# First queries, keys and pooling by 256-column products read by parity, with other places for the pooling weights and a later bias table

## The chip, the cores and the metric

The kernel runs on one core of a Trainium2 chip. The metric is the device time of the program in microseconds. The engines are PE (matrix products, with its own weight loads), ACT, DVE, POOL and SP; SP and POOL also issue transfers (DMA).

## The reference

A bidirectional encoder of two layers over 256 tokens of 1024 channels, in float32. Each layer has two parts:

```python
def _token_mixer(xn, w_in, w_pool, pool_scale, w_a, w_b, w_o, rel_bias):
    u, q, k, v, g_pool, g_attn = jnp.split(xn @ w_in, SPLITS, axis=-1)
    ug = u.reshape(B, S, POOL_GROUPS, POOL_GROUP_DIM)
    pooled = jnp.stack([_centred_mean(ug[:, :, gi], w) for gi, w in enumerate(POOL_WINDOWS)], axis=2) - ug
    pool_out = jnp.einsum('bsgc,gcd->bsgd', pooled, w_pool).reshape(B, S, POOL_WIDTH) * pool_scale
    ...
    for gi, (window, dilation) in enumerate(ATTN_GROUPS):     # (128, 1), (512, 4), (2048, 16), 4 heads each
        ...
        bias = rel_bias[buckets][:, hs].T
        o_g, lse_g = _dilated_group(q[:, :, hs], k[:, :, hs], v[:, :, hs], bias, window, dilation)
    ...
    merged = jax.nn.sigmoid(g_pool) * (pool_out @ w_a) + jax.nn.sigmoid(g_attn) * (attn_out @ w_b)
    return merged @ w_o

def _conv_ffn(xn, w_up, conv_w, conv_b, w_down):
    a, gval = jnp.split(xn @ w_up, 2, axis=-1)
    ...                                                      # depthwise convolution of width 3 on a
    return (jax.nn.gelu(a) * gval) @ w_down
```

Both parts are added to the stream after an RMS norm at their entry, and a last RMS norm ends the program.

## The kernel before

Every float32 operand of a large product is split into a high part, rounded to `fp32r`, and a low part, the rest. A product is then three: high by high, high by low, low by high. The tokens are kept by parity: axis `t` holds even and odd tokens, axis `m` the 128 of each.

The weights are streamed. The class `Weights` holds a list of loads (`add`) and a list of pieces in the order of use (`use`). A load is mostly 1 MB into one of three `raw` buffers, cut into two pieces; a load with a `tag` goes to an idle place named by that tag instead. Opening a piece is a cast on ACT (`wh`, L215) and a subtraction on DVE (`wl`, L216), into one of five pairs of buffers; pieces are opened up to three ahead of the one in use. `load(upto)` issues loads on SP's queue, and `due` says how far ahead that goes.

One layer of the mixer runs as follows. `by_rows` computes 512 columns over four pieces, 48 products of 512 columns, for the pooling branch (`u`), then for two sets of queries and keys (`qk1`, `qk2`): 24 pieces. Its results lie with tokens on the partitions, so they are transposed in blocks on DVE and their blocks exchanged by 16 transfers on POOL's queue (`cross`). After each piece `early` is called; it counts the pieces, moves the exchanges on, and from pieces 15, 17, 19 and 21 on runs the four pooling groups (`pool`: copies of `u` on ACT, running sums on DVE, a split in high and low). Then come eight projections (`proj`, in two pairs of queries and keys for the first head group), and after each of the first four a part of the pooling product (`pool_out`, 12 products). From the seventh on, scores and the rest of the attention are mixed in.

In `proj` the high and low parts of `x` are one operand of 512 columns:

```python
        for k in range(nk):
            nc.tensor.matmul(ps, wh(k), x2[:, k], start=(k == 0), stop=False)
        for k in range(nk):
            nc.tensor.matmul(ps[:, 1], wl(k), x2[:, k, 0], start=False, stop=(k == nk - 1))
```

so two sums come out, and its eviction needs one ACT and two DVE instructions. In other places (`moving`, L90) an operand is read with its two halves in alternation.

In layer 0 only, `load_bias` and `build_bias` make the table `bt` of the attention's position bias: three products from a one-hot matrix (`ohr`, in place `m2`), copies to `fsb`, three transfers to DRAM (`fd`) and five back (`bt`), all on POOL's queue. `build_bias` is a generator that `early` steps, one step for each count above 1: after pieces 2, 3 and 4 a product each, then the transfers. The instruction order on PE, ACT and DVE is that of the source from the end of `u` on; before that, and on POOL and SP throughout, a planner sets it.

Of the kernel before, what the change touches and what calls it, by code (L numbers as in the profile page):

```python
# [10 lines left out]
F32 = mybir.dt.float32  # L11
F32R = mybir.dt.float32r
AF = mybir.ActivationFunctionType
ALU = mybir.AluOpType
AX = mybir.AxisListType

P = 128
D = 1024
S = 256
DEPTH = 2  # L20
KD = D // P
# [12 lines left out]
NT = 5  # L34
# [76 lines left out]
class Weights:  # L111
# [42 lines left out]
    def load_by(self, n):  # L154
# [10 lines left out]
        for c in range(0, shape[0], step):  # L165
            self.nc.sync.dma_start(out=t[:, c : c + step], in_=src[:, c : c + step])
            yield

    def queue_behind(self, insts, n):

        self.behind, self.n_behind = insts, self.n_split + n

    def _split(self, upto):
        nc = self.nc
        self.load(self.due)
        first = self.n_split
        while self.n_split < len(self.pieces):
            i = self.n_split
            n, cut, shape, slot = self.pieces[i]
            if i >= upto and (slot is None or i >= max(upto, first + 2) or i >= upto + 4 or i < 4):  # L180
                break
            if slot is None and len(self.live) == self.BUFS:
                break
            self.load(n + 1)
            with ExitStack() as queued:
                if i < self.n_behind:
                    for inst in self.behind:
                        queued.enter_context(self.tc.issue_after(inst.ins))
                for part in self.open_next():
                    for make in part:  # L190
                        make()
            self.due = n + self.RAW

    def open_next(self):

# [50 lines left out]
def encoder(ctx, tc, x, w_in, w_pool, pool_scale, w_a, w_b, w_o, norm1, norm2, w_up, conv_w,  # L246
# [29 lines left out]
    for l in range(DEPTH):  # L276
        if l == 0:
            slots = (("m2", 0, 2), ("m2", 1, 2), ("ybig",), ("at2",))
            for j in range(2):
                kept = rows(w_in[l], j * 512, 4, C_V, 512)  # L280
                more = rows(w_in[l], j * 512, 4, C_V + 512, 512, "k1" if j else None)
                for n in range(2):
                    W.use(kept[n : n + 1], slots[2 * j + n : 2 * j + n + 1])
                    W.use(more[n : n + 1])
            W.n_scaled = len(W.pieces)
        else:
            W.use(rows(w_in[l], 512, 4, C_V, 512), (("ybig",), ("at2",)))
            for j in range(2):
                W.use(rows(w_in[l], j * 512, 4, C_V + 512, 512))

        def half_of(w, c0, half, n):
            for j in range(n):
                W.use(rows(w, j * 512, 4, c0 + half.start, 512))

        for half in HALVES:
            half_of(w_in[l], 0, half, 2)
        for c0 in (C_Q + 512, C_K + 512, C_Q + 1024, C_K + 1024):
            half_of(w_in[l], c0, HALVES[0], 2)
        for c in PAIRS:
            q = cols(w_in[l], C_Q + c * 256)  # L300
            k = cols(w_in[l], C_K + c * 256)
            if c == 0:
                pool = W.add(
                    w_pool[l].rearrange("g (k p) c -> p (g k) c", p=P), (8, 256),
                    [((lambda t, j=j: t[:, 4 * j : 4 * j + 4, :]), (4, 256)) for j in range(2)],
                )
                q.insert(1, pool[0])
                k.insert(1, pool[1])
            W.use(q + k)
        half_of(w_in[l], C_V + 1024, HALVES[0], 2)  # L310

        for half in HALVES:
            half_of(w_in[l], C_GP, half, 2)
        for half in HALVES:
            half_of(w_a[l], 0, half, 2)
            half_of(w_in[l], C_GA, half, 2)
            half_of(w_b[l], 0, half, 1)
        for c in range(4):
            W.use(rows(w_o[l], c * 256))
        slots = (("v1",), ("ybig",), ("at2",))  # L320
        for kind, n in ORDER.split():
            n = int(n)
            if kind == "v":
                if l + 1 < DEPTH:
                    W.use(rows(w_in[l + 1], 0, 4, C_V, 512), (("m2", 0, 2), ("m2", 1, 2)))
                continue
            for j in range(2):
                if kind == "d":
                    W.use(rows(w_down[l], (4 * n + 2 * j) * P))
                elif kind == "r":  # L330
                    src = w_up[l][j * 512 : (j + 1) * 512].rearrange("(k p) c -> p k c", p=P)
                    c0 = (4 * n * P, 4 * n * P + DFF)
                    W.use(
                        W.add(
                            tuple(src[:, :, c : c + 256] for c in c0), (4, 2, 256),
                            [
                                ((lambda t, j=j: t[:, 2 * j : 2 * j + 2].rearrange("p k h c -> p k (h c)")), (2, 512))
                                for j in (0, 1)
                            ],
                        )  # L340
                    )
                else:
                    p = rows(w_up[l], j * 512, 4, (kind == "g") * DFF + 4 * n * P, 512)
                    W.use(p, slots[2 * j : 2 * j + 2] if (kind, n) == ("a", 0) else ())
        W.use(rows(w_down[l], (NF - 2) * P))
# [76 lines left out]
    def load_bias():  # L422
# [14 lines left out]
        nc.vector.tensor_sub(  # L437
            out=rr[64:96], in0=rb[64:96], in1=rr[64:96].bitcast(F32)
        )
        ohr = big.tile([P, NT * 256], F32R, tag="m2", name="onehot_r")  # L440
        nc.scalar.copy(out=ohr, in_=oh)
        return rr, ohr

    def build_bias(rr, ohr):

        fsb = big.tile([96, NT * 256], F32, tag="q1", name="fsb")
        for c0, groups in ((0, (0, 0)), (512, (0, 1)), (1024, (2,))):
            width = 256 * len(groups)
            ps = acc.tile([P, 512], F32, tag="acc", name="f_ps")
            nc.tensor.matmul(ps[:, :width], rr, ohr[:, c0 : c0 + width], start=True, stop=True)  # L450
            for j, g in enumerate(groups):
                cc = slice(j * 256, (j + 1) * 256)
                rows = slice(32 * g, 32 * g + HPG)
                nc.vector.tensor_copy(fsb[rows, c0 + j * 256 : c0 + (j + 1) * 256], ps[rows, cc])
            yield
# [92 lines left out]

    def chunk_mm(ps, wh, wl, xh, xl, nk):

        for k in range(nk):
            nc.tensor.matmul(ps, wh(k), xh[:, k], start=(k == 0), stop=False)
            nc.tensor.matmul(ps, wh(k), xl[:, k], start=False, stop=False)
            nc.tensor.matmul(ps, wl(k), xh[:, k], start=False, stop=(k == nk - 1))

    def two_sums(ps, wh, wl, x2, nk):


        for k in range(nk):
            nc.tensor.matmul(ps, wh(k), x2[:, k], start=(k == 0), stop=False)  # L560
        for k in range(nk):
            nc.tensor.matmul(ps[:, 1], wl(k), x2[:, k, 0], start=False, stop=(k == nk - 1))

    def proj(x2):

        i, (wh, wl) = W.get()
        flush()
        ps = mmp.tile([P, 2, S], F32, tag="mm", name="proj_ps")
        two_sums(ps, lambda k: wh[:, k, :], lambda k: wl[:, k, :], x2, KD)
        W.free(i)  # L570
        return ps[:, 0], ps[:, 1]

    def halves(a):

        return a.rearrange("p (t m) -> p t m", t=2)

    def in_order(a):

        return a.rearrange("p (m t) -> p t m", t=2)

    def add_up(out, sums):

        nc.scalar.copy(out=out, in_=sums[1])
        nc.vector.tensor_add(out=out, in0=sums[0], in1=out)

    def row_mm(ps, ah, al, wh, wl, first, last):

# [343 lines left out]
    for l in range(DEPTH):  # L931
# [109 lines left out]
        def early():  # L1041
            nonlocal count
            count += 1
            if l == 0 and count > 1:
                next(bias, None)
            if crossing and next(crossing[0], "end") == "end":
                crossing.pop(0)
# [15 lines left out]
        def pool_out(po2):  # L1063
            for j in range(2):
                i, (wh, wl) = W.get()
                for gg in range(2):
                    ph, pl = pooled[2 * j + gg]
                    for oc in range(2):
                        ps = acc.tile([P, 2, P], F32, tag="acc", name="pool_ps")
                        cc = slice(oc * P, (oc + 1) * P)  # L1070
                        chunk_mm(
                            ps, lambda k: wh[:, 2 * gg + k, cc], lambda k: wl[:, 2 * gg + k, cc], ph, pl, 2
                        )
                        c = 4 * j + 2 * gg + oc
# [153 lines left out]
        scaling = scaled_queries()  # L1228
        for c in PAIRS:
            for n in range(4):  # L1230
                src, rest = (halves(a) for a in proj(x2))
                if c == 0:
                    next(pool_parts)
                hd = 2 * c + n % 2
                scale = HD**-0.5 if n < 2 else 1.0
                hi, lo = ((qh, ql) if n < 2 else (kh, kl))

                def evict(hi=hi, lo=lo, hd=hd, scale=scale, src=src, rest=rest):
                    nc.scalar.mul(out=hi[:, hd], in_=src, mul=scale)
                    nc.vector.scalar_tensor_tensor(  # L1240
                        out=lo[:, hd], in0=src, scalar=scale, in1=hi[:, hd].bitcast(F32),
                        op0=ALU.mult, op1=ALU.subtract,
                    )
                    nc.vector.scalar_tensor_tensor(
                        out=lo[:, hd], in0=rest, scalar=scale, in1=lo[:, hd].bitcast(F32),
                        op0=ALU.mult, op1=ALU.add,
                    )

                later.append(evict)
# [305 lines left out]
```

## Time and profile before

| | |
|---|---|
| median of 3 runs | 821.38 us (820.81 to 821.65) |
| the profiled execution | 821.03 us |
| its span, from the first to the last instruction | 819.3 us |
| PE busy | 811.5 us (99%) |
| PE's weight loads busy | 715.0 us (87%) |
| DVE busy | 651.6 us (80%) |
| ACT busy | 481.1 us (59%) |
| POOL busy | 209.5 us (26%) |
| mean granted clock of PE | 0.999 |

A row of a timeline gives the start in us, the time in us, engine, line, operation, output and inputs, shape, how often, and in brackets the idle time before it and what ended that. A row by groups gives line, engine, operation, shapes and count, then busy us in total and mean ns of one. A row of a stretch gives its bounds, its length, and for each engine the busy us with the count of instructions.

### The profile page before, as it was taken

Reading aid. Unit: us, or ns where it says so; the run is one execution under the profiler, and the core shown is the slowest. Engines: PE = TensorE matmul, PEld = TensorE weight load, DVE = VectorE, ACT = ScalarE, POOL = GpSimd, SP = SyncE. Lnnn points to the kernel's source line nnn. Section 1 sums busy time; section 2 is a strip of 40 time slices with the busy share of each in tenths; the row PEclk is TensorE's granted clock in tenths of the full one; section 3 lists DMA queues with packets and bytes.
Section 4 is the critical chain, followed back from the end, with each engine's and each line's share of the span. In section 5 each row is a group of like instructions: output and inputs, shape, how many; then the busy total and the mean of one; then the engine's idle time right before and its main releaser. Section 6 shows DMA issues by size and latency. Waiting matters only on the chain. (4 is left out here: it accounts for less than half of the span.)

```text
span 819.3 us, 11339 instructions
## 1 busy us (share of the span) xinstructions
PE 811.5 (99%) x4030; PEld 715.0 (87%) x4030; DVE 651.6 (80%) x918; ACT 481.1 (59%) x700; POOL 209.5 (26%) x439
## 2 busy tenths in 40 slices
PE   9999999999999999999999999999999999999997
PEld 7888899898888888888888889888888888888886
DVE  6967979667768699989756599796678767999894
ACT  7735475454545577768445456655445447777672
POOL 1153220513012233370000333025030133332501
PEclk9999999999999999999999999999999999999999
DMA  8697585976657888786726776658567487887751
GB/s 316 233 329 227 185 276 169 268 219 220 222 201 237 282 254 256 208 272 211 257 104 212 254 252 201 210 184 258 202 230 258 146 276 237 256 250 236 222 202 52
DMA packets 95164, 186.07 MB, mean 227 GB/s; under 512 B 9774, under 2 KB 26366, under 8 KB 95108
## 3 DMA queue, kind: packets, MB, share of 16 engines
q1 hardware_dynamic: 81956, 160.62, 58.9%
q0 software_dynamic: 12848, 24.43, 10.7%
q8 instruction: 32, 0.52, 0.3%
q10 hardware_dynamic: 304, 0.30, 0.1%
q14 instruction: 24, 0.20, 0.1%
HBM read 160.65 MB, written 1.59 MB: 198 GB/s over the span
## 5 line engine op out<-in xcount | busy, mean ns | idle before, releaser
L216 DVE TENSOR_TENSOR wl<-raw,wh 128x1024 fp32r<-128x1024 f32 x278 | 336.1, 1217 | 112.2 <-ACT wh L215 110.6
L694 PE MATMUL rows_ps<-wh,x 128*128 128x512 f32 x1344 | 405.4, 380 | 0.0
L215 ACT CAST wh<-raw 128x1024 fp32r<-128x1024 f32 x278 | 286.7, 1043 | 141.2 <-PE rows_ps L694 97.0
L694 PEld LDWEIGHTS rows_ps<-wh,x 128*128 128x128 f32 x1344 | 254.1, 189 | 35.6
L694 PE MATMUL rows_ps<-wl,x 128*128 128x512 f32 x672 | 254.7, 379 | 0.0
L694 PEld LDWEIGHTS rows_ps<-wl,x 128*128 128x128 f32 x672 | 127.1, 189 | 17.6
L719 POOL DMA_DIRECT2D up_turned<-up_rows x192 | 94.1, 498 | 164.7 <-DVE up_rows L729 66.0
L588 PE MATMUL res_ps<-wh,actq 128*128 128x512 f32 (+1 forms) x152 | 56.0, 369 | 0.0
L589 PE MATMUL res_ps<-wl,actq 128*128 128x512 f32 (+1 forms) x152 | 55.9, 368 | 0.0
L590 PE MATMUL res_ps<-wh,actk 128*128 128x512 f32 (+1 forms) x152 | 55.9, 368 | 0.0
L719 POOL DMA_DIRECT2D pt<-rows x64 | 31.8, 504 | 80.2 <-ACT wh L215 64.2
L719 POOL DMA_DIRECT2D qk<-qk_rows x64 | 31.3, 497 | 65.6 <-DVE qk_rows L729 30.8
L694 PE MATMUL rows_ps<-wh,po 128*128 128x512 f32 x128 | 39.7, 382 | 0.0
L492 POOL TENSOR_SCALAR ss<-ss 128x1 f32<-128x1 f32 x8 | 1.8, 222 | 133.6 <-ACT junk L488 133.6
L560 PE MATMUL proj_ps<-x,wh 128*128 128x512 f32 x128 | 32.2, 394 | 0.0
L589 PEld LDWEIGHTS res_ps<-wl,actq 128*128 128x128 f32 x152 | 28.8, 189 | 3.7
L588 PEld LDWEIGHTS res_ps<-wh,actq 128*128 128x128 f32 x152 | 28.8, 189 | 3.7
L590 PEld LDWEIGHTS res_ps<-wh,actk 128*128 128x128 f32 x152 | 28.8, 189 | 3.6
L719 POOL DMA_DIRECT2D way<-way x32 | 15.7, 497 | 60.6 <-DVE way L1325 57.9
L719 POOL DMA_DIRECT2D u<-u x32 | 15.8, 502 | 48.4 <-DVE u L729 41.6
L729 DVE STREAM_TRANSPOSE up_rows<-rows_ps 128x512 f32<-128x512 f32 x40 | 26.3, 693 | 2.3 <-PE rows_ps L694 2.3
L1422 ACT ACTIVATE yg<-a,prm 128x256 f32<-128x256 f32 x44 | 26.5, 601 | 1.4
(231 smaller groups left out, 1189.3 us busy)
## 6 DMA issues: line engine op xcount, KB each, us to landing
raw<-in_w_in_dram SPq DMA_DIRECT2D x56, 1024.0 KB, 5.8
raw<-in_w_up_dram SPq DMA_DIRECT2D x40, 1024.0 KB, 5.1
raw<-in_w_down_dram SPq DMA_DIRECT2D x22, 1024.0 KB, 4.8
up_turned<-up_rows POOLq DMA_DIRECT2D x160, 64.0 KB, 5.1
raw<-in_w_a_dram SPq DMA_DIRECT2D x8, 1024.0 KB
raw<-in_w_o_dram SPq DMA_DIRECT2D x8, 1024.0 KB, 4.5
qk<-qk_rows POOLq DMA_DIRECT2D x64, 64.0 KB, 5.0
pt<-rows POOLq DMA_DIRECT2D x64, 64.0 KB, 5.0
```

The source lines that it names most:

```text
L215: lambda: nc.scalar.copy(out=h, in_=src),
L216: lambda: nc.vector.tensor_sub(out=l, in0=src, in1=h.bitcast(F32)),
L492: nc.gpsimd.tensor_scalar_add(ss[:, 3:4], ss[:, 0:1], EPS)
L560: nc.tensor.matmul(ps, wh(k), x2[:, k], start=(k == 0), stop=False)
L588: nc.tensor.matmul(ps, ah, wh, start=first, stop=False)
L589: nc.tensor.matmul(ps, ah, wl, start=False, stop=False)
L590: nc.tensor.matmul(ps, al, wh, start=False, stop=last)
L694: nc.tensor.matmul(ps, x2[:, 2 * n + j, part, t, :], moving(w[:, j], HALVES[0]), start=(n + m == 0), stop=(n == of - 1 and m == 5),)
L719: nc.gpsimd.dma_start(out=out[b, i], in_=in_[a, j])
L729: nc.vector.transpose(out=out[:, :, t].rearrange("p j (a c) r -> p a c j r", a=2), in_=ps[t].rearrange("p (c j r a) -> p a c j r", a=2, c= ...
L1422: nc.scalar.activation(y, aj, AF.Identity, bias=b, scale=w1)
```

## The change

The eight projections and the pooling products use one helper, `chunk_mm`: per 128 channels three products of 256 columns, which read even and odd tokens alternately. One sum comes out, in the order of the tokens, which the eviction reads by parity; its second DVE instruction goes. The pooling weights, one load of 1 MB before, become two of 512 KB, each into an idle place (`q0`, `k0`), and stand in the list of loads ahead of the last two loads of the second key set. `reach` replaces a fixed number of loads ahead: loads to idle places don't count. The one-hot matrix goes to `q0` and `k0` instead of `m2`, in two copies, and the bias steps come for counts above 4 instead of above 1.

```diff
+    def reach(self, n):
+
+        free = self.RAW
+        while n < len(self.loads):
+            free -= self.loads[n][2] is None
+            n += 1
+            if not free:
+                break
+        while n < len(self.loads) and self.loads[n][2] is not None:
+            n += 1
+        return n
...
-            self.due = n + self.RAW
+            self.due = max(self.due, self.reach(n))
...
-        for c0 in (C_Q + 512, C_K + 512, C_Q + 1024, C_K + 1024):
+        for c0 in (C_Q + 512, C_K + 512, C_Q + 1024):
             half_of(w_in[l], c0, HALVES[0], 2)
+        pool = [
+            W.add(
+                w_pool[l].rearrange("g (k p) c -> p (g k) c", p=P)[:, 4 * j : 4 * j + 4], (4, 256),
+                [(lambda t: t, (4, 256))], tag,
+            )
+            for j, tag in enumerate(("q0", "k0"))
+        ]
+        half_of(w_in[l], C_K + 1024, HALVES[0], 2)
...
-        ohr = big.tile([P, NT * 256], F32R, tag="m2", name="onehot_r")
-        nc.scalar.copy(out=ohr, in_=oh)
+        ohr = [
+            big.tile([P, n], F32R, tag=tag, name="onehot_r") for tag, n in (("q0", 1024), ("k0", 256))
+        ]
+        nc.scalar.copy(out=ohr[0], in_=oh[:, 0:1024])
+        nc.scalar.copy(out=ohr[1], in_=oh[:, 1024:])
...
     def chunk_mm(ps, wh, wl, xh, xl, nk):
+        xh, xl = (a.rearrange("p k t m -> p k m t") for a in (xh, xl))
         for k in range(nk):
             nc.tensor.matmul(ps, wh(k), xh[:, k], start=(k == 0), stop=False)
             nc.tensor.matmul(ps, wh(k), xl[:, k], start=False, stop=False)
             nc.tensor.matmul(ps, wl(k), xh[:, k], start=False, stop=(k == nk - 1))
+        return ps.rearrange("p (m t) -> p t m", t=2)
...
-        ps = mmp.tile([P, 2, S], F32, tag="mm", name="proj_ps")
-        two_sums(ps, lambda k: wh[:, k, :], lambda k: wl[:, k, :], x2, KD)
+        ps = mmp.tile([P, S], F32, tag="mm", name="proj_ps")
+        sums = chunk_mm(ps, lambda k: wh[:, k, :], lambda k: wl[:, k, :], x2[:, :, 0], x2[:, :, 1], KD)
...
-            if l == 0 and count > 1:
+            if l == 0 and count > 4:
                 next(bias, None)
...
-                    nc.vector.scalar_tensor_tensor(
-                        out=lo[:, hd], in0=rest, scalar=scale, in1=lo[:, hd].bitcast(F32),
-                        op0=ALU.mult, op1=ALU.add,
-                    )
```

More of the change, by code (lines that the diff above doesn't have):

```diff
@@ L302, in encoder @@
             if c == 0:
-                pool = W.add(
-                    w_pool[l].rearrange("g (k p) c -> p (g k) c", p=P), (8, 256),
-                    [((lambda t, j=j: t[:, 4 * j : 4 * j + 4, :]), (4, 256)) for j in range(2)],
-                )
-                q.insert(1, pool[0])
-                k.insert(1, pool[1])
+                q[1:1], k[1:1] = pool
             W.use(q + k)
@@ L449, in build_bias @@
             ps = acc.tile([P, 512], F32, tag="acc", name="f_ps")
-            nc.tensor.matmul(ps[:, :width], rr, ohr[:, c0 : c0 + width], start=True, stop=True)
+            row, at = ohr[c0 // 1024], c0 % 1024
+            nc.tensor.matmul(ps[:, :width], rr, row[:, at : at + width], start=True, stop=True)
             for j, g in enumerate(groups):
@@ L554, in chunk_mm @@
             nc.tensor.matmul(ps, wl(k), xh[:, k], start=False, stop=(k == nk - 1))
[L556 to L562, printed above, removed]
+        return ps.rearrange("p (m t) -> p t m", t=2)
     def proj(x2):
@@ L567, in proj @@
         flush()
-        ps = mmp.tile([P, 2, S], F32, tag="mm", name="proj_ps")
-        two_sums(ps, lambda k: wh[:, k, :], lambda k: wl[:, k, :], x2, KD)
+        ps = mmp.tile([P, S], F32, tag="mm", name="proj_ps")
+        sums = chunk_mm(ps, lambda k: wh[:, k, :], lambda k: wl[:, k, :], x2[:, :, 0], x2[:, :, 1], KD)
         W.free(i)
[L571 to L584, printed above, removed]
+        return sums
     def row_mm(ps, ah, al, wh, wl, first, last):
@@ L1068, in pool_out @@
                     for oc in range(2):
-                        ps = acc.tile([P, 2, P], F32, tag="acc", name="pool_ps")
+                        ps = acc.tile([P, S], F32, tag="acc", name="pool_ps")
                         cc = slice(oc * P, (oc + 1) * P)
-                        chunk_mm(
+                        ps = chunk_mm(
                             ps, lambda k: wh[:, 2 * gg + k, cc], lambda k: wl[:, 2 * gg + k, cc], ph, pl, 2
@@ L1230, in encoder @@
             for n in range(4):
-                src, rest = (halves(a) for a in proj(x2))
+                src = proj(x2)
                 if c == 0:
@@ L1236, in encoder, with evict @@
                 hi, lo = ((qh, ql) if n < 2 else (kh, kl))
-                def evict(hi=hi, lo=lo, hd=hd, scale=scale, src=src, rest=rest):
+                def evict(hi=hi, lo=lo, hd=hd, scale=scale, src=src):
                     nc.scalar.mul(out=hi[:, hd], in_=src, mul=scale)
@@ L1242, in evict @@
                         op0=ALU.mult, op1=ALU.subtract,
-                    )
-                    nc.vector.scalar_tensor_tensor(
-                        out=lo[:, hd], in0=rest, scalar=scale, in1=lo[:, hd].bitcast(F32),
-                        op0=ALU.mult, op1=ALU.add,
                     )
```

## Prediction

> **What bounds the kernel now.** I read the summary first, then the groups of instructions by shape, then the timeline of each engine around the places that the diff touches.
>
> ```profile
> span 819.3 us, 11339 instructions
> PE 811.5 (99%) x4030; PEld 715.0 (87%) x4030; DVE 651.6 (80%) x918; ACT 481.1 (59%) x700; POOL 209.5 (26%) x439
> ```
>
> PE (matrix products) is busy 811.5 of 819.3 us, so the bound is PE's own rate, and a product saved shortens the run as long as nothing behind PE is late. The profiled execution took 821.03 us, 1.73 more than its span and 0.35 less than the median of 821.38; I sum against 821.03 and add 0.35 at the end. The rate of a product is read from starts, since modelled durations overlap:
>
> ```profile
> 512.19 2.00 PE L560 MATMUL proj_ps<-x,wh 128*128 128x512 f32 x8
> 514.98 2.00 PE L560 MATMUL proj_ps<-x,wh 128*128 128x512 f32 x8
> 498.05 0.28 PE L552 MATMUL pool_ps<-plh,wh 128*128 128x256 f32 x1
> 499.49 2.00 PE L560 MATMUL proj_ps<-x,wh 128*128 128x512 f32 x8
> 407.78 0.27 PE L588 MATMUL res_ps<-wh,actq 128*128 128x256 f32 x1
> 409.00 0.28 PE L590 MATMUL res_ps<-wh,actk 128*128 128x256 f32 x1
> 812.64 0.39 PE L639 MATMUL res_ps<-seed,one_r 128*128 128x256 f32 x2
> 812.87 0.28 PE L588 MATMUL res_ps<-wh,actq 128*128 128x256 f32 x1
> ```
>
> One projection (8 products of 512 columns, 8 of 256, both read straight) takes 514.98 - 512.19 = 2.79 us. Twelve pooling products of 256 columns, read straight, take 1.44 us: 0.120 each. The residual products of 256 columns, which read two halves alternately, stand 11 starts apart in 1.22 us: 0.111 each, with one weight load each as well. L639 also reads alternately, at the very distance (128 elements) that the change uses, and takes 0.115.
>
> **The change, part by part.** *Projections* (16, 8 a layer): 24 products at 0.111 are 2.67 us against 2.79, -0.126 each, -2.0 us in all. At 0.115 the saving would be only 0.03 each (-0.5); at the straight 0.120 it would be a loss of 0.09 each (+1.4). I take 0.111, since 11 intervals carry it and L639 has two. *Pooling* (96 products): 0.0088 each, -0.8 us; nothing at 0.120.
>
> The Trainium skill ("SBUF — State Buffer", section "Door 1: The DMA port swizzle") speaks against this: it says that a read that goes to a new 16-byte line with each element pays, so reading by parity should be the slower of the two. The trace disagrees where it can be compared (0.111 against 0.120 us); by that rule the two parts would come to the +1.4 us above.
>
> *Evictions*: the third DVE instruction goes, and it isn't on the path at the place that matters, as the next part shows:
>
> ```profile
> L1244 DVE SCALAR_TENSOR_TENSOR qkl<-proj_ps,qkl x16: 424/424/427, 102.2 to 528.4; 128x256 fp32r<-128x256 f32 x16
> ```
>
> Columns: shortest, median and longest in ns, first and last start in us. 16 x 0.424 = 6.8 us of DVE, the first only at 102.2; I count 0. If DVE were late only there, it would be worth up to 0.43 a projection.
>
> *Bias table later.* In layer 0 PE waits for the bias row:
>
> ```profile
> 34.59 0.38 PE L694 MATMUL rows_ps<-wl,x 128*128 128x512 f32 x1
> 35.85 0.47 PE L450 MATMUL f_ps<-onehot_r,rr 128*128 128x512 f32 x1 [0.88 <-DVE rr L437]
> 35.42 0.28 DVE L437 TENSOR_TENSOR rr<-rb,rr 32x128 fp32r<-32x128 f32 x1
> 40.49 0.28 PE L450 MATMUL f_ps<-onehot_r,rr 128*128 128x256 f32 x1
> 41.95 0.42 DVE L454 COPY fsb<-f_ps 4x256 f32<-4x256 f32 x1
> 61.53 1.05 ACT L215 CAST wh<-raw 128x1024 fp32r<-128x1024 f32 x1 [1.54 <-PE rows_ps L694]
> 64.12 1.05 ACT L215 CAST wh<-raw 128x1024 fp32r<-128x1024 f32 x1 [1.54 <-PE rows_ps L694]
> ```
>
> Starts are 0.22 apart, so the bias product was due at 34.81 and came at 35.85: 1.04 us lost. One piece takes 64.12 - 61.53 = 2.59 us; from the count's threshold 1 to 4 it is three pieces, 7.8 us, later, and its row (ready at 35.70) is no longer late: -1.04. Splitting the one-hot copy in two costs ACT one more start, some 0.2 us, with no one waiting for 7 us.
>
> What is moved with it is POOL's queue:
>
> ```profile
> 39.38 1.03 POOL L460 DMA_DIRECT2D fd<-fsb  x2 [8.77 <-DVE fsb L454]
> 42.67 0.50 POOL L460 DMA_DIRECT2D fd<-fsb  x1 [2.27 <-DVE fsb L454]
> 44.38 3.06 POOL L463 DMA_DIRECT2D bt<-fd  x4 [1.21 <-DMA fd<-fsb]
> 48.64 0.75 POOL L463 DMA_DIRECT2D bt<-fd  x1 [1.19 <-DMA fd<-fsb]
> 52.70 3.98 POOL L719 DMA_DIRECT2D u<-u  x8 [3.31 <-ACT wh L215]
> 58.49 0.98 POOL L719 DMA_DIRECT2D u<-u  x2 [1.81 <-DMA u<-u]
> 68.50 0.88 ACT L988 COPY u<-u 128x256 f32<-128x256 f32 x2 [3.33 <-DMA u<-u]
> 69.20 1.98 ACT L215 CAST wh<-raw 128x1024 fp32r<-128x1024 f32 x2
> ```
>
> Eight bias transfers stand in POOL's program ahead of the 16 that turn `u`, and each later step waits for the transfers before (5.0 us from the first `fd` to the first `bt`). They end at 49.39. Shifted by 7.8 - 1.04 they end at 56.1, or some 1.3 earlier if the DVE copies queue less (after the third product it took from 40.49 to 42.37): 54.8 to 56.1. `u` can then start 2.2 to 3.5 us later than at 52.70. Besides, the ninth `u` transfer waited for an earlier one (58.49, 5.8 after the first), so eight are open at a time; with `bt` transfers, which take 7.0 us (median) to land, among the eight, I add 0.7 to 1.1. `u` comes D = 2.9 to 4.6 us later; I take 3.9. From below D is -1.0 (POOL serves `u` first and PE is early); from above 7, if the pooling weights (next part) add theirs.
>
> ```profile
> DMA to landing us min/median/max: 4.2/7.0/7.9
> ```
>
> ACT already waits 3.33 us for `u`, and all weight casts behind it in its order wait too. Does PE notice?
>
> ```profile
> 70.27 1.23 DVE L216 TENSOR_TENSOR wl<-raw,wh 128x1024 fp32r<-128x1024 f32 x1 [3.80 <-ACT wh L215]
> 70.00:94.00 24.00, 24.00 (x112) 20.94 (x111) 23.38 (x42) 12.81 (x18) 7.82 (x16) 1.00 0.60 187
> 94.58 1.22 DVE L216 TENSOR_TENSOR wl<-raw,wh 128x1024 fp32r<-128x1024 f32 x1
> 96.65 2.00 PE L560 MATMUL proj_ps<-x,wh 128*128 128x512 f32 x8
> 98.49 1.12 PE L562 MATMUL proj_ps<-x,wl 128*128 128x256 f32 x8
> ```
>
> From `u`'s arrival DVE is packed (23.38 of 24.00 us between 70 and 94), so the low part of the second query piece, done at 95.80, moves one for one with `u`. PE needs it now at 98.49, slack 2.69. After the change PE is there earlier (second projection at 96.65 - 1.04 - 0.13 - 0.11 = 95.37), and `chunk_mm` reads the low part as its third product, 0.22 in, instead of after eight: 95.59. So 0.2 us is lost even with `u` on time, and 0.2 + D with `u` late: 4.1. That is the price of the bias move; the 3.31 us in which POOL sat idle before `u` are the cover that goes.
>
> *Pooling weights* in two loads, ahead of the last key rows:
>
> ```profile
> 85.79 0.37 SPq L150 DMA_DIRECT2D raw<-in_w_pool_dram  x1
> 90.93 2.00 ACT L215 CAST wh<-raw 128x1024 fp32r<-128x1024 f32 x2 [2.20 <-DMA raw<-in_w_pool_dram]
> 92.55 1.22 DVE L216 TENSOR_TENSOR wl<-raw,wh 128x1024 fp32r<-128x1024 f32 x1
> ```
>
> ACT's 2.20 us wait goes, but DVE was packed until 92.55 and would not have started sooner: 0. One more issue costs SP 0.37 us, behind its own waits for free buffers. `q0` and `k0` are written as `qh` only after the weights there are split, long before. The megabyte now moves beside `u`, which is the second rival's ground.
>
> *Layer 1* has no bias. There the low part of the second query piece comes early enough:
>
> ```profile
> 495.76 1.22 DVE L216 TENSOR_TENSOR wl<-raw,wh 128x1024 fp32r<-128x1024 f32 x1
> 519.37 1.34 ACT L1211 ACTIVATE qk<-qk 128x256 f32<-128x256 f32 x4 [3.79 <-DMA qk<-qk_rows]
> 521.15 0.39 PE L1105 MATMUL s_ps<-qk,qk 128*128 128x128 f32 x2
> ```
>
> Done at 496.98, needed at 499.49 - 0.23 + 0.22 = 499.5. The scores need the first of four scaled keys (519.37 + 0.4 = 519.8) at 521.15 less the 1.3 gained by then: 519.9, just in time. Layer 1's half of the product savings, 1.4 us, stands.
>
> *Sum*: -2.0 - 0.8 - 1.04 = -3.9; +4.1 for the late `u`; +0.2. 821.03 + 0.2 + 0.35 = 821.6 us. Its own range, over D from 2.9 to 4.6 and a little around it, is 820.0 to 822.9.
>
> **Rivals.** *`u` isn't late*: POOL's order is not pinned as PE's, ACT's and DVE's are, so `u` may go ahead of the bias, or the bias transfers land faster. Against it: all eight are ready first by the rows above. Then only 0.2 is lost: 821.03 - 3.7 + 0.35 = 817.7 us, faster. The Trainium skill ("DMA: Bandwidth & Descriptors", section "Anatomy of one DMA — SWDGE (gpsimd) path") gives a fixed cost of some 2 us to such a transfer, which would bring the bias table out of the way in time; here the `fd` step took 5.0 us, so I leave this rival second.
>
> *The megabyte of pooling weights holds `u` back further*: a load of this size takes 90.93 - 85.79 = 5.1 us, and it now falls between about 55 and 61 us. Sharing the transfer engines it costs `u` up to half of that, D = 6.0 to 6.5, a loss of 6.2 to 6.7 and +2.3 to +2.8: 823.9 us, slower. It decides from D = 5.3 on, where 3.9 - 0.2 - D passes -1.6. For it: the queues are busy there; against it: `u` moves only 64 KB at a time.
>
> *Reading by parity brings nothing* at 128 elements: +1.4 - 1.04, and the late `u` partly: some 824 us, slower.
>
> **How the numbers follow.** A change within 0.2% (1.6 us) is about what a measurement of this kernel can't tell from none. Late `u` 0.42, `u` not late 0.35, megabyte 0.18, no gain from parity 0.05. Nearly all of the first lies within 0.2%, a little on the fast side: faster 0.36, same 0.41, slower 0.23. The range reaches to both neighbours, 817.5 to 823.9.
>
> **What would show it.** Right: projections 2.67 us apart, pooling products 0.111; no wait before the first bias product; POOL's first `u` near 55 to 56; ACT's wait for `u` near 7 us instead of 3.33; PE idle some 4 us in layer 0 around 90 to 97; layer 1 shorter by 1.4. Wrong: `u` issued by 53, or PE without a gap there; then it is 818. A rate of 0.120 would undo the first two terms.

## The result and the profile after

The changed kernel takes 824.22 us (median of 8 runs, 822.72 to 827.19) against 821.29 for the kernel before in the same comparison (8 runs, 820.81 to 822.26). The ratio is 1.0041, 95% interval 1.0032 to 1.0050: slower by 0.41%, above the predicted range. The profiled execution of the changed kernel took 823.63 us, 2.60 more than the one before (821.03).

The summary of the profile after:

```profile
span 821.8 us, 11577 instructions
PE 810.9 (99%) x4158; PEld 719.0 (87%) x4158; DVE 645.4 (79%) x902; ACT 481.8 (59%) x701; POOL 209.2 (25%) x439
```

PE is busy 0.6 us less in a span that is 2.5 us longer: time went into waits of PE. These are the waits of PE (who waits, for whom: us in total, times, longest; `wl` is the low part of a weight piece):

```profile
PE pool_ps L575 <- DVE wl L228: 1.7, 1, 1.7
PE gain_ps L416 <- DVE mhalf L405: 1.0, 1, 1.0
PE rows_ps L695 <- DVE wl L228: 1.0, 2, 0.6
PE proj_ps L575 <- DVE wl L228: 0.8, 2, 0.4
PE s_ps L1106 <- ACT qk L1212: 0.3, 1, 0.3
```

`gain_ps` was there before; the wait for the bias row `rr` is gone; 3.5 us of waits for low parts `wl` are new, and 0.3 for a key of the scores. Four places tell where the difference arises: the first projection of layer 0, the first row product (`rows_ps`) behind the first two groups of scores, and the same in layer 1. Rows of PE's timeline before:

```profile
92.41 0.62 PE L560 MATMUL proj_ps<-x,wh 128*128 128x512 f32 x2
122.06 0.46 PE L694 MATMUL rows_ps<-wh,x 128*128 128x512 f32 x1
495.26 0.63 PE L560 MATMUL proj_ps<-x,wh 128*128 128x512 f32 x2
524.90 0.46 PE L694 MATMUL rows_ps<-wh,x 128*128 128x512 f32 x1
```

and after:

```profile
90.88 0.48 PE L695 MATMUL rows_ps<-wl,x 128*128 128x512 f32 x1 [0.60 <-DVE wl L228]
93.35 0.27 PE L573 MATMUL proj_ps<-x,wh 128*128 128x256 f32 x1
94.12 0.38 PE L575 MATMUL proj_ps<-x,wl 128*128 128x256 f32 x1 [0.38 <-DVE wl L228]
98.73 0.38 PE L575 MATMUL pool_ps<-plh,wl 128*128 128x256 f32 x1 [1.67 <-DVE wl L228]
100.76 0.38 PE L575 MATMUL proj_ps<-x,wl 128*128 128x256 f32 x1 [0.42 <-DVE wl L228]
125.54 0.46 PE L695 MATMUL rows_ps<-wh,x 128*128 128x512 f32 x1
498.73 0.27 PE L573 MATMUL proj_ps<-x,wh 128*128 128x256 f32 x1
501.41 0.28 PE L573 MATMUL pool_ps<-plh,wh 128*128 128x256 f32 x1
502.75 0.28 PE L573 MATMUL proj_ps<-x,wh 128*128 128x256 f32 x1
527.05 0.46 PE L695 MATMUL rows_ps<-wh,x 128*128 128x512 f32 x1
```

The lag is +0.94 us at the first projection, +3.48 after layer 0's scores, +3.47 when layer 1 begins, +2.15 after its scores: layer 0 loses 3.5, layer 1 gains 1.3. Some 0.35 us more arise later, and I did not trace them. A projection takes 501.41 - 498.73 = 2.68 us (2.79 before), the 12 pooling products 1.34 us (1.44), 0.112 us a product.

Rows of POOL's queue, where the bias table stands ahead of `u`, with the first copy of `u` on ACT and the low part of the second query piece on DVE:

```profile
50.52 3.80 POOL L482 DMA_DIRECT2D bt<-fd  x5 [1.71 <-DMA fd<-fsb]
54.30 1.54 POOL L720 DMA_DIRECT2D u<-u  x3
57.25 0.50 POOL L720 DMA_DIRECT2D u<-u  x1 [1.41 <-DMA bt<-fd]
60.83 0.50 POOL L720 DMA_DIRECT2D u<-u  x1 [1.54 <-DMA bt<-fd]
62.28 3.50 POOL L720 DMA_DIRECT2D u<-u  x7 [0.95 <-DMA bt<-fd]
67.87 0.50 POOL L720 DMA_DIRECT2D u<-u  x1 [0.72 <-DMA u<-u]
73.60 0.87 ACT L989 COPY u<-u 128x256 f32<-128x256 f32 x2 [9.41 <-DMA u<-u]
99.48 1.22 DVE L228 TENSOR_TENSOR wl<-raw,wh 128x1024 fp32r<-128x1024 f32 x1
```

`u`'s first transfer is issued at 54.30 (52.70 before), ACT copies `u` at 73.60 (68.50 before), and the second query piece's low part starts at 99.48 (94.58). After three transfers of `u` POOL stops: four of the next five wait for a bias transfer `bt` to land, 4.3 us in all. Eight are open at a time, and five of the places were taken by `bt`, which moves 256 KB a transfer against 64 KB for `u`. `u`'s last transfer is issued at 67.87, 13.6 us after its first. Before, that took 10.0 us:

```profile
62.73 0.50 POOL L719 DMA_DIRECT2D u<-u  x1 [0.23 <-DMA u<-u]
```

From the last issue to ACT's copy it is 5.7 us after and 5.8 before, and a transfer of `u` lands after 5.8 and 5.7 us (medians). So the 3.5 us that `u` takes longer arise while it is issued, not while it moves. In the trace's view of `bt`:

```profile
DMA to landing us min/median/max: 6.4/6.5/8.4
```

### The profile page after: what moved, and what is told of

It reads as the page before. It is cut to its first block, busy times and chain, and to the rows that moved or that the text cites. A ratio compares the mean times of both kernels' runs of the same rounds, so it can differ in the third digit from the quotient of the medians.

```text
span 821.8 us, 11577 instructions
## 1 busy us (share of the span) xinstructions
PE 810.9 (99%) x4158; PEld 719.0 (87%) x4158; DVE 645.4 (79%) x902; ACT 481.8 (59%) x701; POOL 209.2 (25%) x439
## 5 line engine op out<-in xcount | busy, mean ns | idle before, releaser
L575 PE MATMUL proj_ps<-x,wl 128*128 128x256 f32 x128 | 35.4, 277 | 0.8 <-DVE wl L228 0.8
L573 PE MATMUL proj_ps<-x,wh 128*128 128x256 f32 x128 | 35.4, 276 | 0.0
L574 PE MATMUL proj_ps<-x,wh 128*128 128x256 f32 x128 | 35.2, 275 | 0.0
```

## The experiments

My theory after this result: the bias table's eight transfers, now just ahead of `u`, cost more of `u`'s time than predicted, and the products and the pooling load are not to blame. The rivals: the pooling megabyte holds `u` back, or products by parity bring less than thought. Medians below are of the comparison's own runs; the kernel before had 821.36, 821.53 and 821.42 us in the three groups of runs, 23 to 28 runs in each.

**Bias at its old place, the rest of the change kept**

```diff
-            if l == 0 and count > 4:
+            if l == 0 and count > 1:
```

> The changed kernel with the bias steps back at counts above 1; everything else as changed. Theory (the bias transfers stand ahead of `u` in POOL's queue): `u` reaches ACT at about 68.5 us again instead of 73.6, PE has no waits for `wl` around 90 to 101 us, the 1.0 us wait for the bias row near 35 us returns, and only the products' gain of 2.9 us is left: 818.4 us (817.8 to 819.2). Rival (the megabyte of pooling weights, moved ahead, holds `u` up): `u` still arrives 3 us or more late, 821 us or more. Rival (reading by parity gains nothing): 821.3.

Measured: 820.22 us (12 runs, 819.11 to 822.21), ratio 0.9982 (0.9973 to 0.9990). Faster than before: the move of the bias table turns the sign. Its profile:

```profile
69.56 0.88 ACT L989 COPY u<-u 128x256 f32<-128x256 f32 x2 [2.31 <-DMA u<-u]
```

`u` comes 4.0 us earlier than in the changed kernel. In this profile (819.12 us, at the fast end of the twelve) two transfers of `u` still wait 2.0 us for `bt`, and `u` comes 1.1 us later than in the kernel before. The time is 1.8 us above the expected: the other parts bring less than I reckoned.

**Bias table behind `u`**: its eight transfers are issued after the 16th of `u`.

```diff
+        while len(exchanged) < 16:
+            yield
+        with tc.issue_after(exchanged[15].ins):
             ... the three fd and five bt transfers
-                nc.gpsimd.dma_start(out=out[b, i], in_=in_[a, j])
+                exchanged.append(nc.gpsimd.dma_start(out=out[b, i], in_=in_[a, j]))
```

> The changed kernel with the bias products as changed (counts above 4), but the eight bias transfers pinned behind the sixteen of `u` on POOL. Theory: POOL's first `u` starts by 52 us, the full gain of 3.9 us less the 0.2 us by which DVE is late anyway: 817.6 us (817.0 to 818.6). If it is the pooling weights' megabyte instead, `u` lands late even so: 820 us or more.

Measured: 818.59 us (7 runs, 817.77 to 820.79), ratio 0.9967 (0.9954 to 0.9979). Faster than both kernels.

```profile
51.38 3.91 POOL L724 DMA_DIRECT2D u<-u  x8 [20.68 <-DVE u L734]
59.37 3.90 POOL L724 DMA_DIRECT2D u<-u  x8 [4.08 <-DMA u<-u]
69.34 0.89 ACT L993 COPY u<-u 128x256 f32<-128x256 f32 x2 [5.19 <-DMA u<-u]
520.12 0.49 PE L1110 MATMUL s_ps<-qk,qk 128*128 128x128 f32 x2 [1.20 <-ACT qk L1216]
```

Now all first eight places go to `u`, and the bias row is not waited for. This execution took 820.34 us, near the longest of the seven; in it PE loses 1.2 us of idle time in layer 1 to a scaled key of the scores that comes late. The bias table can stand later than the change puts it; it only must not stand just ahead of `u`.

**The bias move alone, on the kernel before**

```diff
-            if l == 0 and count > 1:
+            if l == 0 and count > 4:
```

with the one-hot copy in two, as in the change.

> The kernel before with the bias change alone: one-hot matrix in `q0` and `k0`, steps at counts above 4. Theory: `u` late by 3 to 4.6 us; of that 0.6 us is slack (the first pooling piece's low part, 93.77 against 95.45 - 1.04), so 2.4 to 4 us are lost and 1.0 gained: 823.0 us (822.2 to 824.3). Rival (the megabyte does it): `u` not late, 820.3.

Measured: 824.89 us (10 runs, 821.79 to 826.88), ratio 1.0039 (1.0027 to 1.0051): this one edit alone loses as much as the whole change. The time is 0.6 us above the expected range.

```profile
54.37 1.55 POOL L723 DMA_DIRECT2D u<-u  x3
73.89 0.88 ACT L992 COPY u<-u 128x256 f32<-128x256 f32 x2 [9.87 <-DMA u<-u]
```

The same picture without the new pooling loads or products: three transfers of `u`, then a stop, and a copy 5.4 us late.

**The old pooling load in the changed kernel** (one load of 1 MB into the ring, at its old place)

```diff
-        pool = [W.add(... [:, 4 * j : 4 * j + 4], (4, 256), ..., tag) for j, tag in enumerate(("q0", "k0"))]
+                pool = W.add(w_pool[l]..., (8, 256), ...)
```

> The changed kernel with the pooling weights in one load of 1 MB in the ring of `raw` buffers and in its old place in the list. Theory: `u` still late, by at most 1.2 us less than in the changed kernel (5.1), so 822.4 to 824.2 us. Rival (the megabyte does it): `u` on time, 817.5 to 818.5.

Measured: 823.87 us (11 runs, 821.83 to 826.64), ratio 1.0028 (1.0018 to 1.0038). Most of the loss stays, so the megabyte isn't what makes the change slow. In its profile (821.83 us, the fastest of the eleven) `bt` lands sooner, after 5.4 to 6.6 us, the waits for it come to 2.6 us instead of 4.3, and ACT copies `u` at 71.53.

**The products alone** (old pooling load, old one-hot copy, bias at its old place)

```diff
-            if l == 0 and count > 4:
+            if l == 0 and count > 1:
```

> The kernel before with the products alone (projections and pooling in 256 columns by parity, one eviction less); bias and pooling weights as before. By 24 products at 0.111 us it gains 2.9 us; `u` comes at 68.5 us and the second query piece's low part 0.8 us ahead of PE: 818.5 us (818.0 to 819.5). If `u` comes later than that in some executions, these lose what goes beyond 0.8 us. Rival (no gain from parity): 821.3.

Measured: 819.84 us (12 runs, 818.73 to 820.69), ratio 0.9978 (0.9969 to 0.9987): -1.7 us, where the prediction's two terms came to -2.8. From first projection to the row product behind the scores layer 1 gains 1.31 us (29.64 to 28.33), layer 0 only 0.61 (29.65 to 29.04): there PE, earlier than before, loses 0.7 us, most of it (0.5) in the first scores, which wait for a scaled key, and the rest at a low part.

**The new pooling loads alone**, on the kernel before (`reach`, two loads into `q0` and `k0`, early):

```diff
-        for c0 in (C_Q + 512, C_K + 512, C_Q + 1024, C_K + 1024):
+        for c0 in (C_Q + 512, C_K + 512, C_Q + 1024):
             half_of(w_in[l], c0, HALVES[0], 2)
+        pool = [...]
+        half_of(w_in[l], C_K + 1024, HALVES[0], 2)
```

> The kernel before with the pooling weights alone moved (two loads into `q0` and `k0`, ahead of the last key rows). Theory: `u` about 1 us later at most (69.6 in the run with the bias back), within the 1.7 us of slack that the old order of products has: 821.3 us (820.9 to 822.2). Rival (the megabyte delays `u` by 3 us or more): 822.7 or more.

Measured: 822.25 us (11 runs, 821.75 to 822.72), ratio 1.0007 (0.9999 to 1.0016): no difference that can be told.

**Bias behind `u`, low products last** (in `chunk_mm` all eight products with `wl` after the sixteen with `wh`), for the claim that reading `wl` third instead of ninth costs:

```diff
+        for k in range(nk):
             nc.tensor.matmul(ps, wl(k), xh[:, k], start=False, stop=(k == nk - 1))
```

> The changed kernel with the bias transfers behind `u`, and in each product of 256 columns the low weights read after all high ones, not as every third product. If reading the low parts early costs (PE at the second query piece 1.6 us earlier than its `wl` allows), the waits for `wl` that are left go, and with them the spread: 817.6 us (817.2 to 818.4), against 818.6 without. If that reading order doesn't matter: 818.6.

Measured: 818.77 us (5 runs, 817.80 to 819.57), ratio 0.9965 (0.9953 to 0.9977), as without it (0.9967). With the bias behind `u` the order of reading is worth nothing measurable.

**Four running sums on POOL instead of DVE**, in the changed kernel, to relieve DVE between 75 and 99:

```diff
-                nc.vector.tensor_add(
+                (nc.gpsimd if gi == 3 else nc.vector).tensor_add(
```

> The changed kernel with the four running sums of the last pooling group on POOL instead of DVE. Theory (DVE is packed from `u`'s arrival, so PE's waits for `wl` are DVE's work): the low parts of the first pooling piece and the second query piece come 2.9 us earlier, and 2 to 2.5 us of PE's waits go: 822.0 us (821.2 to 823.0). Rival (ACT's casts, not DVE, hold PE up): 824.2.

Measured: 828.17 us (5 runs, 827.41 to 829.34), ratio 1.0083 (1.0071 to 1.0096). Wrong in sign. Its timeline of POOL and DVE:

```profile
96.71 4.43 POOL L996 TENSOR_TENSOR us<-us 128x538 f32<-128x538 f32 x3 [0.73 <-DVE pll L1019]
101.17 0.18 DVE L1005 TENSOR_TENSOR us<-us,edge 128x16 f32<-128x16 f32 x1 [3.48 <-POOL us L996]
102.07 1.22 DVE L228 TENSOR_TENSOR wl<-raw,wh 128x1024 fp32r<-128x1024 f32 x1
```

DVE waits 3.48 us for POOL, in its fixed order, and the low part comes at 102.07 instead of 99.48, 2.6 us later. It was no relief, but it tells the same of the chain. The profiled execution (827.41 us) is 3.8 us longer than that of the changed kernel, and the other 1.2 us are PE's own. Its product that reads this low part, and a stretch behind it (bounds, length, busy us and count of PE, its weight loads, DVE, ACT and POOL, then the clock granted to PE as a share of the full one, the share of the DMA engines and GB/s):

```profile
103.35 0.58 PE L575 MATMUL proj_ps<-x,wl 128*128 128x256 f32 x1 [3.98 <-DVE wl L228]
104.00:105.00 1.00, 1.00 (x6) 1.00 (x6) 1.00 (x2) 1.00 (x2) 0.00 (x0) 0.50 0.39 86
```

Behind the wait of 3.98 us the granted clock is 0.50 up to about 106.4, and the twelve products from 103.72 to 106.28 take 2.56 us instead of 1.34. In the changed kernel, whose longest wait there is 1.67 us, it stays at 1.00 from 95 to 105. That the wait brought the lower clock about is suggested by this one profile, not shown.

**Bias one piece later** (threshold 2) **and two pieces later** (threshold 3), to see whether the cost grows piece by piece:

```diff
-            if l == 0 and count > 4:
+            if l == 0 and count > 2:
```

> The changed kernel with the bias steps at counts above 2, one piece later than in the kernel before instead of three. Theory: the bias transfers end by about 51 us, when `u` is ready, so `u` comes as with the bias back (69.6 us); the wait for the bias row goes (1.0 us), but DVE's low parts come no sooner, so PE waits for them instead and little is won over the bias back (820.2): 820.0 us (819.2 to 820.8). Rival (each piece of shift costs the same, 4 us over three): 821.5.

> The changed kernel with the bias steps at counts above 3, two pieces later than in the kernel before. Theory: past the 3.3 us for which POOL was idle ahead of `u`, each piece of 2.6 us puts `u` off by as much; with two pieces the bias transfers end some 1.5 to 2 us after `u` is ready: 821.9 us (820.9 to 823.0), between 820.0 and the changed kernel's 824.2.

Measured: 823.33 us (12 runs, 821.81 to 826.06), ratio 1.0024 (1.0014 to 1.0033), and 823.38 us (11 runs, 822.03 to 824.23), ratio 1.0019 (1.0010 to 1.0028). A cost by the piece falls: one piece costs as much as two. POOL's timeline with one piece later shows why it is no smaller dose:

```profile
48.65 0.80 POOL L482 DMA_DIRECT2D bt<-fd  x1 [5.58 <-DMA fd<-fsb]
49.45 0.51 POOL L479 DMA_DIRECT2D fd<-fsb  x1
56.67 3.64 POOL L720 DMA_DIRECT2D u<-u  x7
75.60 0.80 ACT L989 COPY u<-u 128x256 f32<-128x256 f32 x2 [10.75 <-DMA u<-u]
```

One `fd` went behind the first `bt`, whose own wait of 5.58 us it then sat out; the last `bt` waits another 3.70 us for it, and `u` starts at 56.67, later than in the changed kernel. (This execution took 826.06 us, the longest of the twelve, so its 75.60 is an upper case.) With two pieces `u` starts at 53.23, but `bt` takes longer to land (6.7 to 9.0 us), its waits come to 5.0 us, and ACT copied `u` at 73.64, as with three.

**Straight reading, bias at its old place** (the sums read accordingly), against the first experiment:

```diff
-        xh, xl = (a.rearrange("p k t m -> p k m t") for a in (xh, xl))
-        return ps.rearrange("p (m t) -> p t m", t=2)
+        return ps.rearrange("p (t m) -> p t m", t=2)
```

> The kernel with the bias back (820.2 us), its products of 256 columns read straight, first the even and then the odd tokens, instead of by parity. If the parity gives the rate: 0.120 instead of 0.111 us a product, 0.2 us more a projection and 0.1 more a pooling part, 4.0 us in all, of which layer 0 swallows up to 0.8 where PE waits for DVE: 823.5 us (822.8 to 824.4). If the rate came from the 256 columns alone: 820.2.

Measured: 823.49 us (8 runs, 823.16 to 825.43), ratio 1.0029 (1.0019 to 1.0039), as expected.

```profile
496.50 0.28 PE L572 MATMUL proj_ps<-x,wh 128*128 128x256 f32 x1
499.38 0.29 PE L572 MATMUL pool_ps<-plh,wh 128*128 128x256 f32 x1
500.82 0.28 PE L572 MATMUL proj_ps<-x,wh 128*128 128x256 f32 x1
```

A projection takes 2.88 us and the 12 pooling products 1.44, 0.120 a product. So the gain of the products is the reading by parity: without it this kernel loses 2.1 us on the kernel before, with it it wins 1.1 (the first experiment), and the products alone win 1.7.

**Bias behind `u` with the old pooling load**

```diff
 (the edit of "Bias table behind u", and that of "The old pooling load")
```

> The kernel with the bias transfers behind `u` (818.6 us), with the pooling weights in one load in their old place. If the megabyte beside `u` costs the 0.4 to 0.8 us that the other pairs of runs show: `u` by 68.5 us instead of 69.3, 818.0 us (817.3 to 818.5). If not, or if the early pooling weights save as much: 818.6 to 819.2.

Measured: 819.03 us (5 runs, 817.42 to 819.41), ratio 0.9961 (0.9949 to 0.9973), as with the new load (0.9967): these two, and the one with the low products last, are the fastest versions, 0.33 to 0.39% below the kernel before.

```profile
51.26 3.92 POOL L721 DMA_DIRECT2D u<-u  x8 [20.71 <-DVE u L731]
55.57 3.92 POOL L721 DMA_DIRECT2D u<-u  x8 [0.39 <-DMA u<-u]
63.92 0.89 ACT L990 COPY u<-u 128x256 f32<-128x256 f32 x2
```

In this execution (817.59 us) the second eight follow after 0.39 us, ACT doesn't wait for `u`, and PE waits for no low part. That is the first rival's 817.7 us, reached in single executions; the median stays 1.3 us above.

## Why the prediction was wrong

*Right*: the chain from the bias transfers over `u`, ACT's casts and packed DVE to PE. Bias first on POOL, `u` issued at 54.30 (predicted near 55 to 56, so a little early), no wait before the bias product, PE idle in layer 0 between 90 and 101 for low parts (3.1 us in the rows above, some 4 predicted), layer 1 shorter by 1.32 (1.4 predicted). ACT's wait for `u` was 9.41 us, where I had it near 7. The rates stand: 2.68 and 1.34 us. By the Trainium skill's rule on 16-byte lines ("SBUF — State Buffer", "Door 1: The DMA port swizzle") reading by parity would have been the slower. The runs go against it: 0.112 against 0.120 us, and 820.22 against 823.49.

*Wrong: the size of D, in its second part.* The prediction split D into a later start of `u` (2.2 to 3.5 us) and 0.7 to 1.1 for bias transfers among the eight open ones. The start was only 54.30 - 52.70 = 1.6 later. From first issue to ACT's copy `u` took 73.60 - 54.30 = 19.3 us, against 68.50 - 52.70 = 15.8: +3.5, three times and more what I allowed. With `u` holding 3 places of 8, its next transfers wait for `bt` landings (4.3 us in four waits, of which the rows above show 1.41, 1.54 and 0.95) and only then begin their own. D is 5.1, not 3.9, and outside the 2.9 to 4.6 that I took for its bounds. I had the row that says how long `bt` takes to land (7.0 us median) and turned it into an added microsecond instead of writing out which transfer of `u` would stand behind which landing. That the places taken by `bt` make these 3.5 us is read from the rows; a run with the bias table issued from another queue, which would isolate it, wasn't made. The other profiles agree where the table stands ahead of `u`: the waits for `bt` and the time from `u`'s first issue to ACT's copy rise together, from none and 15.8 to 16.7 us (before, the products alone, the new pooling loads alone) over 2.0 and 17.4 (bias back) and 2.6 and 17.1 (old pooling load) to 4.0 and 19.5 (bias move alone) and 5.0 and 20.4 (two pieces later). With the table behind `u` it took 18.0, 18.3 and 12.7 us without any such wait, so other things move it too.

The Trainium skill ("DMA: Bandwidth & Descriptors", "Anatomy of one DMA — SWDGE (gpsimd) path") counts a fixed cost of some 2 us for such a transfer. Here `bt` landed after 6.4 to 8.4 us, so the rival that I drew beside that page, `u` not late, had no ground as long as the bias stood first.

*Wrong: the wait of the scores.* I had the scores just in time in layer 1 and priced nothing for them in layer 0, where PE now waits for a scaled key (timeline after):

```profile
120.74 0.28 PE L1101 MATMUL s_ps<-kh,qh 128*128 128x256 f32 x1
121.34 1.33 ACT L1212 ACTIVATE qk<-qk 128x256 f32<-128x256 f32 x4 [5.25 <-DMA qk<-qk_rows]
121.81 0.49 PE L1106 MATMUL s_ps<-qk,qk 128*128 128x128 f32 x2 [0.32 <-ACT qk L1212]
122.05 0.36 PE L573 MATMUL proj_ps<-x,wh 128*128 128x256 f32 x1
```

This first group of scores takes 122.05 - 120.74 = 1.31 us; before, it took 118.45 - 117.73 = 0.72:

```profile
117.73 0.28 PE L1100 MATMUL s_ps<-kh,qh 128*128 128x256 f32 x1
118.45 2.09 PE L560 MATMUL proj_ps<-x,wh 128*128 128x512 f32 x8
```

In the products alone too, layer 0 gives back 0.7 of its gain. The product terms (-2.8) were right as rates and 1.1 us too large as a gain (-1.7 measured alone): 0.7 of it because in layer 0 PE, being earlier, meets inputs that are not ready. The rest is open but for some 0.15 of the rates.

At layer 1's start the prediction's own terms (-1.4, -1.04, +4.1) come to +1.7; measured +3.5. Of the 1.8 between, 1.1 is D: the low part came 4.9 us later, and PE read it at 100.76, where the terms put it at 95.59 + 4.1 = 99.7. Another 0.6 is the scores' wait, and the small rest is the rates (0.11 and 0.10 instead of 0.126 and 0.11).

*The rivals.* The time came out where the rival of the pooling megabyte had it (823.9), but that is luck, not its mechanism: with the old load the ratio is 1.0028, and without the megabyte early the same `u` is late in the bias move alone. I had put the pooling loads at zero. In each of four pairs the kernel with the new loads has the higher ratio (1.0041 against 1.0028, 0.9982 against 0.9978, 0.9967 against 0.9961, 1.0007 against 1): 0.3 to 1.1 us, no pair by itself beyond its intervals, and the second differs in the place of the one-hot matrix too. A cost of about half a microsecond is suggested, not shown.

*Open*: why the median with the bias behind `u` stays some 1 us above its best execution. In the three profiles of such kernels ACT copied `u` at 69.34, 69.81 and 63.92, and PE waited 1.2, 0.6 and 0 us for a key of the scores, in executions of 820.34, 819.48 and 817.59 us. That fits, but it is one profile of each. Open too is why the changed kernel spreads more than the one before (822.72 to 827.19 against 820.81 to 822.26). It isn't the products: alone they spread from 818.73 to 820.69, and the bias move alone, with the old products, from 821.79 to 826.88. In the changed kernel the two longest executions (826.15 and 827.19) had a mean granted clock of 0.997, the six others 0.998 or 0.999; with the bias move alone it was 0.997 in four of ten (825.04 to 826.88). A clock of 0.50 for 3 us, as with the sums on POOL, lowers the mean by 0.002, so a longer wait of PE in these executions would do it. No profile of one of them was taken, so this is not shown.

## What to carry to other kernels

When work is moved on a queue, price not only its issue but the places that its transfers hold: the next user of the queue starts a little later and then waits for their landings. A wait of 1 us at its engine can cost less than the place its cure is moved to; put the moved transfers behind the urgent ones, not between the last idle time and them. And a saving on the bounding engine counts only where its inputs have slack: read that stage by stage before multiplying a rate by a count.

## What was not expected of the hardware

- POOL took 4.43 us for three sums of 128x538, about 1.5 each, where DVE takes 2.20 for three (before, its timeline):

```profile
90.43 2.20 DVE L995 TENSOR_TENSOR us<-us 128x538 f32<-128x538 f32 x3
```

- With eight transfers of POOL's queue open, four of the five landings of the bias table (6.4 to 8.4 us after the issue) became waits of `u`'s next transfers. Whether the chip or the program's own semaphores set the eight, no run shows.
- Products of 256 columns read alternately at 128 elements take 0.112 us in the projections and the pooling, close to the residual products (0.111, alternately at 256 elements), against 0.120 read straight.
- With the sums on POOL, PE's granted clock was 0.50 for some 3 us behind a wait of 3.98 us, and products stood 0.21 us apart instead of 0.112. In the changed kernel it was 1.00 behind a wait of 1.67 us.
